# A decoder block on one core: up projection with both halves of the activations in one matmul, convolution over three blocks at a time, merge projections with tokens on the partition

## The chip, the core and the metric

The kernel runs on one core of a Trainium2 chip. The core has a matrix engine (PE, with its weight loads shown apart as PEld), a vector engine (DVE), a scalar engine (ACT), GpSimd (POOL) and a queue engine (SP) that issues most transfers. Matmul results go to PSUM; everything else lies in SBUF with 128 partitions. The metric is the device time of one execution in microseconds (us), and lower is better. [...]

## What is computed

One decoder layer for 256 tokens of 2048 channels, batch 1 (cut to what matters):

```python
h = rmsnorm(x, norm1_g) * (1 + sc1) + sh1            # sh1, sc1, g1, sh2, sc2, g2 = silu(c) @ w_ada + b_ada
proj = h @ w_in        # queries, keys, values, gates, GLU input (a, g), merge gates (ga, gb)
o_nsa = nsa_attention(q, kc, vc, ks, vs, kw, vw)     # 16 heads of 128, two key/value groups
y_a = o_nsa @ w_o_nsa
u = a * sigmoid(g)
u = causal_dwconv(u, conv_dw_w, width 31) + conv_dw_b
y_b = silu(layernorm(u)) @ conv_pw_w + conv_pw_b
merged = sigmoid(ga) * y_a + sigmoid(gb) * y_b
x = x + g1 * (merged @ w_out)
h = rmsnorm(x, norm2_g) * (1 + sc2) + sh2
u = causal_dwconv(h @ ffn_w_up, ffn_dw_w, width 3) + ffn_dw_b     # 2 * 5632 columns: a, g
x = x + g2 * ((silu(g) * a) @ ffn_w_down)
out = rmsnorm(x, final_g)
```

## The kernel before

The weights of the products, nearly 300 MB, are read once, in tiles of 128 partitions by up to 1024 columns (`wtile`, L202 to L215): SP issues the transfer of `raw`, ACT casts it to `hi` (L212), DVE subtracts to get `lo` (L213). `hi` and `lo` have three buffers each, so a cast waits until PE has finished with the tile three before it. (Up to the attention a fourth pair, from the pool `more`, takes every fourth tile.) Each product runs over the contraction in blocks of 128 (k) and holds its result in one of two PSUM accumulators.

There are two forms of product. `prod_x` puts tokens on the partition of the result: the activations are the loaded operand, the weights stream, up to 512 columns in one matmul, and each k takes 2 token blocks x 3 matmuls (L235 to L237). `prod_w` puts channels on the partition: 128 columns of weights are the loaded operand and the activations stream, 256 columns (the tokens), so that 512 columns of weights take 4 blocks x 3 matmuls for each k (L249, L251, L252). Activations are kept as two tiles, one of hi and one of lo.

The order of the work is that of the code, with three queues of background work (`heads_q`, `conv_q`, `ada_q`): after each weight tile `tick` takes items from them, as long as the costs written beside an item (ns of DVE, ACT, transfer) stay under what PE has been given. The instructions are then put in order at build time, for each engine apart, by a scheduler; weight casts have priority. On the chip each engine follows its own list in order.

The stages, with the time at which the first matmul of each starts: the shift and scale and the first GLU blocks (0 to 180 us), the rest of the GLU, keys, values and the first queries (to 416 us), the attention of 16 heads among the products of `q_chunk(2)`, `q_chunk(3)` and `gate_a` (to about 626 us), w_o_nsa, the gates gb and conv_pw_w (to 908 us), w_out (to 1013 us), and the feed-forward part in three pieces of up and down projection (to the end).

The depthwise convolution of 31 taps is background work from 182 us to 691 us: for each pair of channel blocks ACT makes the first term and DVE adds 30 taps to each block by one multiply-add over 256 tokens each (L446). The layer norm over channels follows, then its result is split into `uT` for conv_pw_w. In the attention, `scores(h)` makes the exponentials of head h and `values(h)` multiplies them with the values; `heads` puts the scores AHEAD = 2 heads before the values. Three of the four gates `gate_a` are made during the attention. The merge adds the two branches, channels on the partition, and splits the sum into `mT`, the loaded operand of w_out. The steps of `ada_steps` (L263 to L269) stream w_ada through DVE for the later shifts, scales and gates.

## Time and profile before

| | |
|---|---|
| three runs | 1781.09, 1782.22, 1783.61 us, median 1782.22 us |
| profiled execution, span from first to last instruction | 1779.5 us (its own time with what lies around the span is not listed) |
| PE busy | 97% of the span, 13252 matmuls |
| DVE busy | 71% |
| ACT busy | 48% |
| read from HBM | 402.80 MB, 228 GB/s over the span |
| granted TensorE clock, mean | 0.986 of full |

A busy time counts every moment in which an instruction of the engine was under way. Matmuls overlap, so the pace of PE is read from the starts of neighbouring matmuls and not from their durations. Idle time of an engine is put down to what ended it.

### The profile page before, as it was taken

The numbers are of one execution on the slowest core, as the hardware profiler recorded it, in microseconds if no ns is written. First come the engines' busy times: TensorE is split into PE (matmuls) and PEld (weight loads), VectorE is DVE, ScalarE is ACT, GpSimd is POOL, SyncE is SP. The second block draws the span as 40 slices with busy tenths as digits, with TensorE's granted clock in tenths as the row PEclk, the third lists the DMA queues.
The fourth block names the chain that finished last, engine by engine and source line by source line (L and its number), as shares of the span: only waits on it lengthen the run. The fifth ranks groups of instructions, "written<-read, shape, count | busy, mean of one in ns | idle before, by whom it ended". The sixth has DMA issues, their size and how long they took to land.

```text
span 1779.5 us, 32395 instructions
## 1 busy us (share of the span) xinstructions
PE 1726.8 (97%) x13252; PEld 1628.7 (92%) x13252; DVE 1268.8 (71%) x1808; ACT 845.5 (48%) x1168; POOL 5.5 (0%) x22
## 2 busy tenths in 40 slices
PE   5999999999999999999999899999999999999997
PEld 3777999899999999999988899998999998999986
DVE  2223999998999898877885666666556766576665
ACT  4333444344768644653344644444344454344453
POOL 0000000000000000000000000000000000000000
PEclk9989999999999999999999999999999999999998
DMA  9996777884764676799997576766676767666663
GB/s 307 358 334 221 225 226 230 272 283 135 240 195 130 210 240 202 243 325 308 308 312 234 177 234 205 219 207 227 207 219 207 220 205 223 206 176 186 181 190 127
DMA packets 225152, 407.01 MB, mean 229 GB/s; under 512 B 12876, under 2 KB 91500, under 8 KB 224364
## 3 DMA queue, kind: packets, MB, share of 16 engines
q1 hardware_dynamic: 223596, 400.49, 71.4%
q10 hardware_dynamic: 1408, 4.46, 0.7%
q8 instruction: 103, 1.69, 0.4%
q14 instruction: 45, 0.37, 0.1%
HBM read 402.80 MB, written 2.10 MB: 228 GB/s over the span
## 4 chain that ended last, share of the span: by engine, by line
PE 91%; DMA 3%; DVE 3%; ACT 1%; issue 1%; SPq 0%; DVEq 0%; ACTq 0%
PE accw L252 20%; PE accw L249 20%; PE accw L251 20%; PE accx L236 6%; PE accx L237 6%; PE accx L235 6%; DMA araw<-in_w_ada_dram 2%; PE pt L664 1%; PE pt L368 1%; DVE lo L213 1%; PE pt L703 1%; PE pt L398 1%; PE pt L399 1%; PE pt L400 1%; PE acc_g L398 1%
## 5 line engine op out<-in xcount | busy, mean ns | idle before, releaser
L212 ACT CAST hi<-raw 128x1024 fp32r<-128x1024 f32 (+2 forms) x562 | 574.5, 1023 | 816.1 <-PE accw L251 474.6
L213 DVE TENSOR_TENSOR lo<-raw,hi 128x1024 fp32r<-128x1024 f32 (+2 forms) x562 | 668.4, 1190 | 408.0 <-ACT hi L212 398.8
L252 PE MATMUL accw<-act,lo 128*128 128x256 f32 x3104 | 883.0, 285 | 1.3 <-DVE lo L213 1.3
L249 PE MATMUL accw<-act,hi 128*128 128x256 f32 x3104 | 882.7, 284 | 0.0
L251 PE MATMUL accw<-act,hi 128*128 128x256 f32 x3104 | 882.5, 284 | 0.0
L252 PEld LDWEIGHTS accw<-act,lo 128*128 128x128 f32 x3104 | 596.1, 192 | 4.1 <-issue 1.8
L249 PEld LDWEIGHTS accw<-act,hi 128*128 128x128 f32 x3104 | 596.4, 192 | 3.4 <-issue 2.6
L251 PEld LDWEIGHTS accw<-act,hi 128*128 128x128 f32 x3104 | 596.3, 192 | 2.4 <-issue 2.2
L236 PE MATMUL accx<-lo,act 128*128 128x512 f32 (+2 forms) x664 | 227.6, 343 | 1.0 <-DVE lo L213 1.0
L235 PE MATMUL accx<-hi,act 128*128 128x512 f32 (+2 forms) x664 | 227.0, 342 | 0.0
L237 PE MATMUL accx<-hi,act 128*128 128x512 f32 (+2 forms) x664 | 226.7, 342 | 0.0
L446 DVE SCALAR_TENSOR_TENSOR cacc<-big,cw,cacc 128x255 f32<-128x255 f32 (+24 forms) x480 | 201.2, 464 | 0.3
L269 DVE SCALAR_TENSOR_TENSOR t<-araw,cs,t 128x1024 f32<-128x1024 f32 x120 | 153.6, 1280 | 23.5 <-DMA araw<-in_w_ada_dram 23.5
L236 PEld LDWEIGHTS accx<-lo,act 128*128 128x128 f32 x664 | 125.8, 189 | 18.4 <-DVE lo L213 2.6
L235 PEld LDWEIGHTS accx<-hi,act 128*128 128x128 f32 x664 | 125.8, 189 | 14.5 <-ACT hi L212 0.2
L237 PEld LDWEIGHTS accx<-hi,act 128*128 128x128 f32 x664 | 125.8, 189 | 14.3 <-issue 0.4
L904 DVE SCALAR_TENSOR_TENSOR t<-accw,fw,t 128x255 f32<-128x255 f32 (+1 forms) x176 | 84.2, 479 | 2.5
L902 ACT ACTIVATE t<-accw,fw 128x256 f32<-128x256 f32 x88 | 49.3, 560 | 0.0
L368 PE MATMUL pt<-araw,cz 128*32 128x256 f32 x512 | 37.4, 404 | 9.7 <-DMA araw<-in_w_ada_dram 7.5
L318 DVE TENSOR_TENSOR act<-t,act 128x512 fp32r<-128x512 f32 x38 | 26.0, 686 | 18.3 <-ACT act L317 18.3
L368 PEld LDWEIGHTS pt<-araw,cz 128*32 128x32 f32 x512 | 12.9, 111 | 20.5 <-DMA araw<-in_w_ada_dram 5.8
L677 ACT ACTIVATE s<-s,st 128x128 f32<-128x128 f32 (+1 forms) x64 | 28.5, 447 | 1.4 <-DVE st L675 1.1
(208 smaller groups left out, 1035.6 us busy)
## 6 DMA issues: line engine op xcount, KB each, us to landing
araw<-in_w_ada_dram SPq DMA_DIRECT2D x192, 512.0 KB, 5.4
raw<-in_ffn_w_up_dram SPq DMA_DIRECT2D x176, 512.0 KB, 3.7
raw<-in_w_in_dram SPq DMA_DIRECT2D x116, 512.0 KB, 4.5
raw<-in_ffn_w_down_dram SPq DMA_DIRECT2D x88, 512.0 KB, 4.6
raw<-in_w_in_dram SPq DMA_DIRECT2D x48, 384.0 KB, 3.8
raw<-in_w_o_nsa_dram SPq DMA_DIRECT2D x32, 512.0 KB, 4.8
raw<-in_conv_pw_w_dram SPq DMA_DIRECT2D x32, 512.0 KB, 6.2
raw<-in_w_out_dram SPq DMA_DIRECT2D x32, 512.0 KB, 5.2
```

The costliest lines, as they stand in the source:

```text
L212: nc.scalar.copy(hi[:, :n], raw[:, :n])
L213: los.append(nc.vector.tensor_tensor(lo[:, :n], raw[:, :n], hi[:, :n], op=ALU.subtract).ins)
L235: nc.tensor.matmul(o, ah[:, k, s], hi, start=k == 0, stop=False)
L236: nc.tensor.matmul(o, ah[:, k, s], lo, start=False, stop=False)
L237: nc.tensor.matmul(o, al[:, k, s], hi, start=False, stop=k == nk - 1)
L249: nc.tensor.matmul(acc[:, b, :], hi[:, s], ah[:, k, :], start=k == 0 and b % 2 == 0, stop=False, skip_group_check=True)
L251: nc.tensor.matmul(acc[:, b, :], hi[:, s], al[:, k, :], start=False, stop=False, skip_group_check=True)
L252: nc.tensor.matmul(acc[:, b, :], lo[:, s], ah[:, k, :], start=False, stop=last, skip_group_check=True)
L269: nc.vector.scalar_tensor_tensor(acc, raw, cs[:, k:k + 1], acc, op0=ALU.mult, op1=ALU.add)
L368: nc.tensor.matmul(p_[32 * i:32 * i + 32, side, :], cz[:, k + i, :], raw[:, i, :], start=k == 0, stop=k == KB - 4, skip_group_check=True)
L446: nc.vector.scalar_tensor_tensor(acc[:, s:], u[:, b, :T - s], cw[:, CW - 1 - s, b:b + 1], acc[:, s:], op0=ALU.mult, op1=ALU.add)
L904: nc.vector.scalar_tensor_tensor(dst[:, j, s:], pp[:, j, :T - s], fw[:, 2 - s, b:b + 1], dst[:, j, s:], op0=ALU.mult, op1=ALU.add)
```

## The change

- `prod_p` is new and makes the up projection: hi and lo of the activations lie side by side in one tile `[P, KB, 2, T]`, so that one matmul of 512 columns takes weights hi x activations (hi | lo), and a second one of 256 columns adds weights lo x activations hi. It makes 256 columns of weights at a time (their transfers have rows of 1 KB instead of 2 KB); hi and lo sums meet in `ffn_conv`, by a copy on ACT and an addition on DVE.
- The four gates ga, w_o_nsa, the four gates gb and conv_pw_w become `prod_x`. The merge has tokens on the partition, takes the bias of conv_pw_w from a transfer that repeats it on all partitions, and is turned by 32 transposes (`turn_m`), three and four weight tiles after the end of each of the four merge products (`coming`).
- The convolution takes three blocks at a time (one group has one block). For 16 of 31 taps (`WIDE`) ACT makes the products of the blocks into one tile `cprod` with a single buffer, and DVE adds it to all three blocks at once; for 14 taps DVE does what it did.
- AHEAD becomes 1. The fourth pair of `hi` and `lo` before the attention is gone. The gate `g1b` gets its place when the convolution is done, and its 32 ada steps enter the queue there at a transfer cost of 1500.

```diff
-AHEAD = 2
+AHEAD = 1
...
-    acts = ctx.enter_context(tc.tile_pool(name="acts", bufs=4))
+    acts = ctx.enter_context(tc.tile_pool(name="acts", bufs=2))
...
-        return acts.tile([P, KB, T], F32R, tag="act", name=nm("act"))
+        return acts.tile([P, KB, 2, T], F32R, tag="act", name=nm("act"))
...
     def tick():
+        for c in coming:
+            c[0] -= 1
+        while coming and coming[0][0] <= 0:
+            coming.popleft()[1]()
...
-        turn[0] += 1
-        pool, bufs = (ext[0], 1) if ext[0] is not None and turn[0] % 4 == 0 else (wp, 3)
-        hi = pool.tile([P, WT], F32R, tag="hi", name=nm("hi"), bufs=bufs)
-        lo = pool.tile([P, WT], F32R, tag="lo", name=nm("lo"), bufs=bufs)
+        hi = wp.tile([P, WT], F32R, tag="hi", name=nm("hi"))
+        lo = wp.tile([P, WT], F32R, tag="lo", name=nm("lo"))
...
+    def prod_p(act, src, c0):
+        acc = ps_acc.tile([P, 2, 2, T], F32, tag="acc", name=nm("accp"))
+        for k, hi, lo in tiles(src, KB, c0, 2 * P):
+            for b in range(2):
+                s = slice(b * P, (b + 1) * P)
+                nc.tensor.matmul(acc[:, b], hi[:, s], act[:, k], start=k == 0, stop=False, skip_group_check=True)
+                nc.tensor.matmul(acc[:, b, 0, :], lo[:, s], act[:, k, 0, :], start=False, stop=k == KB - 1,
+                                 skip_group_check=True)
+        return acc
...
+    WIDE = (3, 5, 7, 9, 11, 13, 15, 17, 19, 21, 23, 25, 27, 29, 30, 1)
...
+        def product(b, s):
+            def f():
+                if b == b0:
+                    box["p"] = cvp.tile([P, n, T], F32, tag="cprod", name=nm("cprod"))
+                    if s == 1:
+                        nc.gpsimd.memset(box["p"][:, :, 0:1], 0.0)
+                nc.scalar.mul(box["p"][:, b - b0, s:], u[:, b, :T - s], cw[:, CW - 1 - s, b:b + 1])
+            return f
+        def wide(s):
+            def f():
+                acc, prod = box["a"], box["p"]
+                if s == 1:
+                    nc.vector.tensor_add(u[:, b0:b0 + n, :], acc, prod)
+                else:
+                    nc.vector.tensor_add(acc[:, :, s:], acc[:, :, s:], prod[:, :, s:])
+            return f
...
+        narrow = deque(({"dve": 470}, tap(b, s)) for s in range(2, CW) if s not in WIDE for b in blk)
+        each = -(-len(narrow) // len(WIDE))
+        for s in WIDE:
+            conv_q.extend(({"act": 500}, product(b, s)) for b in blk)
+            conv_q.extend(narrow.popleft() for _ in range(min(each, len(narrow))))
+            conv_q.append(({"dve": 170 + n * 265}, wide(s)))
...
-        gp = prod_w(h1, w_in, C_MA + n * 512, 512)
+        gp = prod_x(h1, w_in, C_MA + n * 512, 512)
...
-        yp = prod_w(oT, w_o_nsa, n * 512, 512)
-        nc.vector.tensor_mul(merged[:, 4 * n:4 * n + 4, :], yp, sg)
+        yp = prod_x(oT, w_o_nsa, n * 512, 512)
+        nc.vector.tensor_mul(merged[:, :, n * 512:(n + 1) * 512], yp, sg)
...
+    def turn_m(b):
+        def f():
+            p_ = pt([P, 2, T])
+            for j in range(2):
+                for t in range(NT):
+                    nc.tensor.transpose(p_[:, j, t * P:(t + 1) * P], merged[:, t, (b + j) * P:(b + j + 1) * P], ident)
+            split(mT[:, b:b + 2], p_)
...
-        yp = prod_w(uT, conv_pw_w, n * 512, 512)
...
+        yp = prod_x(uT, conv_pw_w, n * 512, 512)
+        y = t4([P, NT, 512])
+        for t in range(NT):
+            nc.vector.tensor_add(y[:, t, :], yp[:, t, :], bias)
+            nc.vector.tensor_mul(y[:, t, :], y[:, t, :], gbs[:, t, s])
+            nc.vector.tensor_add(merged[:, t, s], merged[:, t, s], y[:, t, :])
+        coming.extend([3 + i, turn_m(4 * n + 2 * i)] for i in range(2))
...
     def ffn_conv(pp, b0, dst):
-        for j in range(4):
+        v = t4([P, 2, T])
+        nc.scalar.copy(v, pp[:, :, 1, :])
+        nc.vector.tensor_add(v, v, pp[:, :, 0, :])
+        for j in range(2):
...
-            pg = prod_w(h2, ffn_w_up, FFN + (b0 + i) * P, 512)
+            pg = prod_p(h2, ffn_w_up, FFN + (b0 + i) * P)
```

Where the instructions stand: first PE in the second product of the up projection, before the change (accw is the accumulator, act the two activation tiles, hi and lo the weights).

```order
L249 MATMUL accw_11472<-act_11107,hi_11474 128x256
L251 MATMUL accw_11472<-act_11108,hi_11474 128x256
L252 MATMUL accw_11472<-act_11107,lo_11475 128x256
L249 MATMUL accw_11472<-act_11107,hi_11474 128x256
L251 MATMUL accw_11472<-act_11108,hi_11474 128x256
L252 MATMUL accw_11472<-act_11107,lo_11475 128x256
```

And the same two blocks after it:

```order
L263 MATMUL accp_9996<-act_9791,hi_9998 128x512
L264 MATMUL accp_9996<-act_9791,lo_9999 128x256
L263 MATMUL accp_9996<-act_9791,hi_9998 128x512
L264 MATMUL accp_9996<-act_9791,lo_9999 128x256
```

Two matmuls of 256 columns have become one of 512, and the third stays.

Second, DVE among the GLU products, where the convolution begins (cacc is its sum, cprod ACT's products, t a sum of ada steps), before:

```order
L213 TENSOR_TENSOR lo_1785<-raw_1783,hi_1784 128x768
L213 TENSOR_TENSOR lo_1813<-raw_1811,hi_1812 128x768
L446 SCALAR_TENSOR_TENSOR cacc_1668<-big_191,cw,cacc_1668 128x253
L446 SCALAR_TENSOR_TENSOR cacc_1674<-big_191,cw,cacc_1674 128x253
L213 TENSOR_TENSOR lo_1839<-raw_1837,hi_1838 128x768
L446 SCALAR_TENSOR_TENSOR cacc_1668<-big_191,cw,cacc_1668 128x252
L446 SCALAR_TENSOR_TENSOR cacc_1674<-big_191,cw,cacc_1674 128x252
L213 TENSOR_TENSOR lo_1869<-raw_1867,hi_1868 128x768
```

After:

```order
L467 SCALAR_TENSOR_TENSOR cacc_1667<-big_190,cw,cacc_1667 128x250 x3
L216 TENSOR_TENSOR lo_1846<-raw_1844,hi_1845 128x768
L486 TENSOR_TENSOR cacc_1667<-cacc_1667,cprod_1787 128x3x249
L216 TENSOR_TENSOR lo_1879<-raw_1877,hi_1878 128x768
L467 SCALAR_TENSOR_TENSOR cacc_1667<-big_190,cw,cacc_1667 128x248 x3
L216 TENSOR_TENSOR lo_1904<-raw_1902,hi_1903 128x768
L486 TENSOR_TENSOR cacc_1667<-cacc_1667,cprod_1870 128x3x247
L216 TENSOR_TENSOR lo_1935<-raw_1933,hi_1934 128x768
```

Every second tap of three blocks is now one addition (L486) that needs ACT's cprod, and it stands between the weight tiles.

Third, PE at the values of the last but two head. Before, it stands among the products of the third gate (L698 to L700 are transposes of the exponentials, L703 and L704 the values, L664 the scores, accw_6516 the gate):

```order
L252 MATMUL accw_6516<-act_189,lo_6755 128x256
L703 MATMUL pt_6057<-t_869_6063,big_3235 128x256
L704 MATMUL pt_6057<-t_869_6063,big_3235 128x128
L664 MATMUL pt_6091<-big_3235,big_3898 128x2x128
L664 MATMUL pt_6093<-big_3235,big_3898 128x512
L703 MATMUL pt_6057<-t_871_6071,big_3235 128x256
L704 MATMUL pt_6057<-t_871_6071,big_3235 128x128
L249 MATMUL accw_6516<-act_189,hi_6754 128x256
L251 MATMUL accw_6516<-act_190,hi_6754 128x256
L695 MATMUL pt_6146<-big_3235 128x256
```

After (L700 scores, L739 and L740 values, accx_6637 the first product with w_o_nsa, act_4631 the heads' results):

```order
L239 MATMUL accx_6637<-hi_6763,act_4631 128x512
L739 MATMUL pt_6073<-t_921_6079,big_3276 128x256
L740 MATMUL pt_6073<-t_921_6079,big_3276 128x128
L700 MATMUL pt_6107<-big_3276,big_3960 128x2x128
L700 MATMUL pt_6109<-big_3276,big_3960 128x512
L739 MATMUL pt_6073<-t_923_6087,big_3276 128x256
L740 MATMUL pt_6073<-t_923_6087,big_3276 128x128
L731 MATMUL pt_6149<-big_3276 128x256
L237 MATMUL accx_6829<-hi_6831,act_4631 128x512
L734 MATMUL pt_6151<-ident,s_6054 128x128
```

Among the values of head 12 stood the scores of head 15, and now stand those of head 14. The third gate has ended by then: the values of all of the last eight heads stand behind it, among the first two products with w_o_nsa, whose k-th block needs the result of head k.

## Rows read from the trace of the kernel before

**Rows 1.** The page: busy time by engine, and TensorE's granted clock in 40 slices.

```profile
PE 1726.8 (97%) x13252; PEld 1628.7 (92%) x13252; DVE 1268.8 (71%) x1808; ACT 845.5 (48%) x1168; POOL 5.5 (0%) x22
...
PEclk9989999999999999999999999999999999999998
```

**Rows 2.** The chain that ended last, shares of the span by engine.

```profile
PE 91%; DMA 3%; DVE 3%; ACT 1%; issue 1%; SPq 0%; DVEq 0%; ACTq 0%
```

**Rows 3.** Timeline of PE in the up projection: start us, duration us, instruction.

```profile
1099.73 0.28 PE L249 MATMUL accw<-act,hi 128*128 128x256 f32 x1
...
1100.69 0.28 PE L252 MATMUL accw<-act,lo 128*128 128x256 f32 x1
```

**Rows 4.** Timeline of PE in the down projection, columns as before.

```profile
1224.78 0.39 PE L236 MATMUL accx<-lo,act 128*128 128x512 f32 x1
...
1226.60 0.39 PE L235 MATMUL accx<-hi,act 128*128 128x512 f32 x1
```

**Rows 5.** Busy time by stage: window, length, engines (instructions), PE clock, DMA share, GB/s.

```profile
165.00:415.00 250.00, 248.00 (x2059) 239.27 (x2060) 222.07 (x389) 109.00 (x135) 1.29 (x4) 0.99 0.78 238
415.83:649.52 233.69, 233.69 (x1762) 222.40 (x1761) 212.27 (x432) 150.04 (x327) 0.53 (x1) 0.99 0.60 187
...
814.55:908.35 93.80, 93.45 (x769) 92.15 (x767) 78.16 (x82) 36.75 (x39) 0.00 (x0) 1.00 0.90 307
...
1012.76:1779.50 766.74, 754.32 (x5563) 721.27 (x5561) 497.58 (x574) 359.73 (x430) 0.00 (x0) 0.99 0.65 200
```

**Rows 6.** The chain in order of time, attention: start us, us, what.

```profile
431.10 0.44 PE pt L645 x4
431.54 1.72 PE pt L664 x6
...
452.68 0.43 PE pt L703 x2
```

**Rows 7.** Groups by line and shape, 415 to 650 us, ACT's work for the heads.

```profile
L677 ACT ACTIVATE s<-s,st 128x256 f32<-128x256 f32 x32 | 15.9, 500 | 0.1
L702 ACT COPY t<-pt 128x384 f32<-128x384 f32 x32 | 14.5, 472 | 9.1 <-PE pt L700 8.9
L693 ACT ACTIVATE s<-s,st 128x256 f32<-128x256 f32 x32 | 14.4, 497 | 0.0
L677 ACT ACTIVATE s<-s,st 128x128 f32<-128x128 f32 x32 | 12.6, 394 | 1.2 <-DVE st L675 1.1
...
L677 ACT ACTIVATION_READ_ACCUMULATOR s<-s,st 128x1 f32 x64 | 12.1, 188 | 0.0
L693 ACT ACTIVATE s<-s,st 128x128 f32<-128x128 f32 x32 | 11.1, 395 | 1.2 <-DVE st L683 1.1
...
L317 ACT CAST act<-pt 128x256 fp32r<-128x256 f32 x16 | 5.9, 369 | 12.5 <-PE pt L704 12.4
```

**Rows 8.** Who waited for whom, 415 to 650 us: total, times, longest.

```profile
ACT hi L212 <- PE accw L251: 44.4, 28, 4.0
```

**Rows 9.** Groups of the whole span, DVE and ACT: busy us, mean ns.

```profile
L212 ACT CAST hi<-raw 128x1024 fp32r<-128x1024 f32 x476 | 499.3, 1050 | 685.5 <-PE accw L251 428.0 <-PE accx L237 165.7 <-issue 72.1
...
L213 DVE TENSOR_TENSOR lo<-raw,hi 128x768 fp32r<-128x768 f32 x48 | 45.6, 954 | 10.0 <-ACT hi L212 6.4 <-PE pt L400 3.3
...
L864 DVE TENSOR_TENSOR big<-big,t 128x512 f32<-128x512 f32 x12 | 8.1, 683 | 0.0
```

**Rows 10.** The page's groups: the taps of the convolution before.

```profile
L446 DVE SCALAR_TENSOR_TENSOR cacc<-big,cw,cacc 128x255 f32<-128x255 f32 (+24 forms) x480 | 201.2, 464 | 0.3
```

**Rows 11.** Transfers from 1200 to 1250 us, rows of 2 KB and more.

```profile
DMA packets 5434, 11.25 MB, mean 225 GB/s; under 512 B 345, under 2 KB 345, under 8 KB 5430
...
q1 hardware_dynamic: 5430, 11.20, 68.6%
```

**Rows 12.** Transfers from 1250 to 1268 us, nearly all rows of 1 KB.

```profile
DMA packets 3605, 4.01 MB, mean 223 GB/s; under 512 B 119, under 2 KB 3454, under 8 KB 3603
...
q1 hardware_dynamic: 3603, 3.98, 70.9%
```

More of the change, by code (lines that the diff above doesn't have):

```diff
@@ L315, in split @@
     def split(dst, src):
-        hi, lo = dst
+        hi, lo = (dst[:, :, 0, :], dst[:, :, 1, :]) if len(dst.shape) == 4 else (dst[:, 0, :], dst[:, 1, :])
         nc.scalar.copy(hi, src)
@@ L397, in glu_first @@
             s = slice(b * P, (b + 1) * P)
-            nc.tensor.matmul(o, hi[:, 0, s], h1[0][:, k, :], start=k == 0 and not second, stop=False, skip_group_check=True)
-            nc.tensor.matmul(o, hi[:, 0, s], h1[1][:, k, :], start=False, stop=False, skip_group_check=True)
-            nc.tensor.matmul(o, lo[:, 0, s], h1[0][:, k, :], start=False, stop=k == KB - 1, skip_group_check=True)
+            nc.tensor.matmul(o, hi[:, 0, s], h1[:, k, 0, :], start=k == 0 and not second, stop=False, skip_group_check=True)
+            nc.tensor.matmul(o, hi[:, 0, s], h1[:, k, 1, :], start=False, stop=False, skip_group_check=True)
+            nc.tensor.matmul(o, lo[:, 0, s], h1[:, k, 0, :], start=False, stop=k == KB - 1, skip_group_check=True)
     with tc.tile_pool(name="first", bufs=4) as first:
@@ L731, in block_kernel, with conv_done @@
         drain(heads_q)
-    late = ctx.enter_context(tc.tile_pool(name="late", bufs=1))
-    g1b = late.tile([P, D], F32, name="gb", tag="gb")
-    for i in range(2):
-        ada_q.extendleft(reversed(ada_steps(2 * D + i * WT, to_bcast(g1b, 2 * D, i), PACE)))
+    gate1 = {}
+    def conv_done():
+        cv.__exit__(None, None, None)
+        late = ctx.enter_context(tc.tile_pool(name="late", bufs=1))
+        gate1["b"] = late.tile([P, D], F32, name="gb", tag="gb")
+        for i in range(2):
+            ada_q.extendleft(reversed(ada_steps(2 * D + i * WT, to_bcast(gate1["b"], 2 * D, i), 1500)))
+    conv_q.append(({}, conv_done))
     lb = {}
```

118 lines of the change are left out of this document (52 added, 66 removed).

## The prediction

> **What bounds the kernel now.** I read the busy times first: PE 97% of the span, DVE 71%, ACT 48%, the clock full in nearly every slice [rows 1]. A busy PE alone proves little, because matmuls overlap; but the chain that ended last runs on PE for 91% of the span [rows 2]. So I looked at PE's pace. In the up projection nine neighbouring matmuls of 256 columns start within 0.96 us, 120 ns apart [rows 3]; in the down projection nine of 512 columns start within 1.82 us, 227 ns apart [rows 4]. So two matmuls of 256 columns cost 240 ns and one of 512 costs 227. A line through both pairs gives 107 ns for 256 columns and 13 ns for each matmul, whatever its length. The stages show no other bound for long: in the last 767 us PE is busy for 754, DVE for 498 and ACT for 360 [rows 5]. Two places are tight besides: the attention (416 to 650 us), where DVE is busy for 212 of 234 us, and 815 to 908 us, where the transfers' share is 0.90 [rows 5].
>
> **The up projection.** 88 blocks of 128 columns times 16 blocks of k are 1408 triples of matmuls. A triple took 3 x 120 = 360 ns; one of 512 columns and one of 256 take 227 + 120 = 347. 13 ns x 1408 = **-18.3 us**. What comes on top lies beside PE: 44 products each get a copy on ACT and an addition of 512 elements on DVE, 0.68 us [rows 9], 30 us in all. DVE then has 498 + 30 of some 748 us, ACT about 360 + 30: cover enough; without it each addition would cost its 0.68 us. The weights now come in rows of 1 KB. The stretch of the down projection that already reads such rows moves 223 GB/s at a share of 70.9% [rows 12], the stretch before it 225 GB/s at 68.6% with longer rows [rows 11]: 4% more engine time for each byte. With the faster PE the last stage's 0.65 [rows 5] becomes 0.65 x 360/347 x 1.04 = 0.70. I cost it at nothing; if it were no longer hidden, PE would wait on transfers at most as now at a share of 0.90.
>
> **Sixteen products with tokens on the partition.** For 512 columns and one k, 12 matmuls of 256 columns (1440 ns) become 6 of 512 (1362 ns): 78 ns, times 16 k, times 16 products: **-20.0 us** (a product falls from 23.0 to 21.8 us). The loaded operand and the streamed one trade places, which rows 3 and 4 show in both forms at these paces.
>
> The trace can be set against a rule here. By the Trainium skill, "TensorE: Matmul & The Clock Gate", section "Back-to-back issue gap", a matmul of N columns at the full clock follows the last after N / 2.4 + 2.5 ns. That would make a matmul less worth 2.5 ns, and the 1408 + 1536 that go worth 7.4 us instead of the 38.3 us above; the sum below would end at 1784 us. The trace does not agree: 120 ns stand where the rule gives 109 [rows 3]. I go by the rows.
>
> **The merge.** 32 transposes come onto PE. Four of 128 columns take 0.44 us [rows 6]: 32 x 0.11 = **+3.5 us** (7 if they fall into a stretch at half clock). They stand three and four weight tiles into the next product, so that PE should not wait for the sum. DVE gets six operations of 512 elements for each merge product, 6 x 0.68 = 4.1 us [rows 9], beside a product of 21.8 us, about what it did before. The transfers there go from 0.90 to 0.90 x 23.0/21.8 = 0.95. Close, but not over; if they bind, the 5 us that the four merge products gain are lost.
>
> **The convolution.** DVE loses 16 of 30 taps of 16 blocks: 480 operations in 201 us become 224, at 0.42 us 94 us [rows 10]. It gains 80 additions over three blocks, 0.95 us each as the subtraction of 768 elements [rows 9], and 16 over one, in all about 82 us. So DVE has some 25 us less. ACT gets 256 products of about 0.5 us, the price of its scaling of 256 elements [rows 7]: 127 us, in a stretch (165 to 650 us) where it has 109 + 150 of 484 us [rows 5]. PE was the bound there already, so I count no gain for DVE's 25 us. The new wait is this: cprod has one buffer, so ACT's next product waits for DVE's addition, and the weight casts stand behind it on ACT. Cover: a cast itself waits for PE to free a buffer (44 us in the attention stretch alone [rows 8]), and two finished tiles lie ahead, over 5 us at 23 us for eight tiles. Cost 0 is my value; the upper bound is a rival below.
>
> **The attention.** Ahead of a head's transposes now stands one head's work less. By the order, the values of all of the last eight heads come after the third gate. From the values of head 8 to those of head 15, PE has 130 matmuls of w_o_nsa products (29.5 us at 227 ns) and some 26 us of the heads themselves (scores of a head 1.29 us, from six for 1.72; values about 2.4 us [rows 6]): 55.5 us. ACT has in the same stretch 12 weight casts at 1.05 us [rows 9], 24 exponentials, 24 reads of their sums, 24 scalings, 16 copies and 8 casts of results at 0.50 and 0.39, 0.19, 0.50 and 0.40, 0.47 and 0.37 us [rows 7], and 18 products of the convolution at up to 0.50: 12.6 + 10.7 + 4.5 + 10.7 + 7.6 + 3.0 + 8.9 = 58 us. So ACT is the longer by 2.5 us, with no waits counted, where before PE was busy throughout [rows 5]. Each head also needs a way round: scores, exponentials on ACT, scalings on ACT, transposes, copies, values. I take **+6 us**; lower bound 0, upper bound 2 us for each of the eight heads, 16 us.
>
> **Sum.** 1779.5 (span) - 18.3 - 20.0 + 3.5 + 6 = 1750.7 us. The span of the profiled execution is 2.7 us under the median of the runs, 1782.2, and I add this as what lies around it: **1753 us**.
>
> **Rivals.**
> - *The forecast*, with the attention at 0 to 14 us and the merge's transfers at 0 to 5: 1747 to 1764. Chance 0.62.
> - *ACT becomes the bound from 165 to 690 us.* For: 127 us more on an engine that follows its list in order, and AHEAD = 1. Against: half of its time was free there, and most of its waiting was for PE. If the attention loses its 16 us and the exchange of products in the convolution another 5 to 10 us, the time is near 1770 (1764 to 1778). Chance 0.17.
> - *Slower: the single cprod buffer.* Each of 96 additions on DVE waits for the last of ACT's products, which waits for the addition before. If 0.5 us of this (one product [rows 7]) shows on PE each time, it is 48 us: 1753 + 48 = 1801. It decides from 29 / 96 = 0.3 us on. For: DVE is busy for 222 of the 250 us from 165 us on, and can make up little. Against: in the order one to two weight tiles (2.2 to 2.9 us of PE) stand between two additions. Chance 0.09.
> - *The fixed cost is not of each matmul.* If the 512-column matmul, between matmuls of 256, starts the next one 240 ns later and not 227, the up projection gains nothing: 1771. Against it stand the starts between neighbours of 512 columns [rows 4]; no row is for it. Chance 0.03.
> - *Better*: no wait at all in the attention, and DVE's 25 us end some of the old ones: under 1747, near 1742. PE has only 2 us idle of 250 ahead of the attention [rows 5], so there is little to end. Chance 0.09.
>
> **How the numbers follow.** About 0.2%, 3.6 us, is what a measurement of this kernel can tell from no change. Faster is the forecast, the better case, the fixed-cost case and nearly all of the second: 0.62 + 0.09 + 0.03 + 0.14 = 0.88. Same, 1778.6 to 1785.8, takes the end of the second: 0.03. Slower: 0.09. The predicted time is that of the likeliest case. The range leaves out the slower case, the end of the second and half of the better one: 1742 to 1775, with some 0.83 inside.
>
> **What would show it.** Right: in the up projection starts 227 and 120 ns apart in turn, and a last stage (from the first up matmul to the end) about 18 us shorter; four gates, w_o_nsa and merge products of 21.8 us where PE does nothing else; DVE under 90% from 165 to 416 us. Wrong: casts on ACT that wait for DVE's additions or for the convolution's products, with PE waiting for lo or hi behind them; PE idle between the heads by more than 2 us each; transposes of the merge at twice their time; weights of the up projection landing late.

## The result and the profile after

The changed kernel takes 1769.8 us in the median of four runs (1767.07 to 1772.41), the kernel before 1781.65 us. The ratio is 0.993, with a 95% interval of 0.9914 to 0.9946; in a second comparison it was 0.9932 (0.9917 to 0.9946). So it is faster, by some 12 us, where the forecast was 29: the time lies inside the range, but at less than half of the gain.

The page of the changed kernel, busy times and the chain that ended last by engine, which answer to [rows 1, 2]:

```profile
PE 1705.5 (96%) x10340; PEld 1476.0 (83%) x10340; DVE 1268.9 (72%) x1692; ACT 968.3 (55%) x1465; POOL 6.1 (0%) x28
...
PE 83%; DVE 6%; DMA 5%; ACT 3%; issue 2%; SPq 0%; DVEq 0%; ACTq 0%
```

PE has some 2900 matmuls less but is busy for only 21 us less, and the chain now leaves PE for 17% of the span instead of 9%. The windows by stage, columns as in [rows 5], cut at the first matmul of the same products; first the rows of the kernel before that [rows 5] leaves out:

```profile
649.52:742.51 92.99, 92.99 (x775) 92.88 (x773) 82.74 (x107) 41.84 (x42) 0.00 (x0) 1.00 0.72 221
742.51:814.55 72.04, 71.13 (x583) 69.97 (x581) 55.71 (x50) 43.05 (x50) 0.00 (x0) 1.00 0.87 305
...
908.35:1012.76 104.41, 98.83 (x545) 85.75 (x543) 71.78 (x98) 47.63 (x67) 0.00 (x0) 0.97 0.77 250
```

And after the change:

```profile
165.00:417.33 252.33, 248.88 (x2065) 239.99 (x2066) 211.54 (x312) 159.03 (x260) 2.25 (x7) 0.99 0.78 235
417.33:656.63 239.30, 233.54 (x1283) 197.92 (x1281) 203.53 (x363) 186.52 (x422) 0.73 (x3) 0.97 0.57 179
656.63:744.69 88.06, 88.06 (x388) 72.97 (x389) 77.87 (x92) 51.38 (x65) 0.10 (x1) 1.00 0.74 231
744.69:820.70 76.01, 69.52 (x293) 55.80 (x292) 61.04 (x55) 43.32 (x50) 0.00 (x0) 0.98 0.90 316
820.70:916.00 95.30, 94.39 (x429) 76.70 (x428) 83.42 (x86) 37.63 (x39) 0.00 (x0) 1.00 0.93 324
916.00:1017.87 101.87, 96.06 (x529) 83.52 (x527) 69.03 (x94) 46.48 (x66) 0.00 (x0) 0.98 0.71 235
1017.87:1770.40 752.53, 739.70 (x4152) 643.95 (x4152) 514.90 (x618) 386.95 (x486) 0.00 (x0) 0.99 0.65 204
```

Set against the same stages of the two profiled executions (1779.5 and 1770.4 us); the last column is a second profiled execution of the changed kernel (`after_again`, 1770.0 us):

| stage | before, us | after, us | difference | by the forecast's terms | after, once more |
|---|---|---|---|---|---|
| to the attention | 415.8 | 417.3 | +1.5 | 0 | 414.7 |
| attention: 5 of the 16 products | 233.7 | 239.3 | +5.6 | -6.2 + 6 | 238.2 |
| the next 4 products | 93.0 | 88.1 | -4.9 | -5.0 | 88.1 |
| merge: 7 products and w_out | 270.3 | 273.2 | +2.9 | -8.8 + 3.5 | 273.3 |
| feed-forward part | 766.7 | 752.5 | -14.2 | -18.3 | 755.7 |

Only the third row came out as forecast, and it is the one stage after the change in which PE is never idle (88.06 of 88.06 us). The misses are 8.2 us in the merge, 5.8 in the attention, 4.1 in the feed-forward part and 1.5 ahead of the attention, where the second execution has none. PE's idle time, the length of a stage less its busy time, grew from nothing to 5.8 us in the attention and from 6.8 to 13.2 us in the merge.

**The up projection.** A product of two float32 operands is summed from hi x hi, hi x lo and lo x hi of their two parts; L263, the matmul of 512 columns of each pair, makes the first two, and L264 the third. A timeline of PE, L263 alone, first in the first piece, then in the second; the outer rows of each are 20 pairs apart:

```profile
1099.92 0.40 PE L263 MATMUL accp<-act,hi 128*128 128x512 f32 x1
...
1106.85 0.40 PE L263 MATMUL accp<-act,hi 128*128 128x512 f32 x1
```

```profile
1399.74 0.40 PE L263 MATMUL accp<-act,hi 128*128 128x512 f32 x1
...
1406.81 0.40 PE L263 MATMUL accp<-act,hi 128*128 128x512 f32 x1
```

6.93 us for 20 pairs is 346.5 ns, as forecast. 7.07 us is 353.5 ns, and it stays so through all 512 pairs of the second piece, with nothing waiting and the clock full. Over the trace, the starts in the first piece follow one another in a cycle of two pairs (231 + 112, 233 + 117 ns), in the third piece of one (230 + 117) and in the second of three (241 + 120, 235 + 114, 232 + 118). The second piece is the one that PE enters straight from the down projection, with nothing between.

**The attention.** PE and ACT in their timelines, from the moment in which PE has nothing more to do (L713 exponentials of the next head, L215 weight casts, L477 products of the convolution, L331 the cast of a finished head's result, L237 the product with w_o_nsa that needs it):

```profile
588.90 0.27 PE L736 MATMUL pt<-ident,s 128*128 128x128 f32 x1
593.78 0.79 PE L237 MATMUL accx<-hi,act 128*128 128x512 f32 x1 [4.60 <-ACT act L331]
```

```profile
587.24 1.28 ACT L713 ACT_TABLE_LOAD   x1
588.53 0.40 ACT L713 ACTIVATE s<-s,st 128x128 f32<-128x128 f32 x1
...
589.32 1.98 ACT L215 CAST hi<-raw 128x1024 fp32r<-128x1024 f32 x2
591.20 0.51 ACT L713 ACTIVATE s<-s,st 128x256 f32<-128x256 f32 x1
...
591.71 0.49 ACT L713 ACTIVATE s<-s,st 128x256 f32<-128x256 f32 x1
...
592.20 1.27 ACT L477 ACTIVATE cprod<-big,cw 128x249 f32<-128x249 f32 x3
593.38 0.35 ACT L331 CAST act<-pt 128x256 fp32r<-128x256 f32 x1
```

ACT does not pause. The 0.35 us cast for which PE waits stands behind a table load, the exponentials of the next head, two weight casts and three products of the convolution. Behind this wait the granted clock was at half, the level of 1.2 GHz, until 600.0 us:

```profile
593.10:600.00 6.90, 6.22 (x15) 4.46 (x16) 3.84 (x11) 4.81 (x15) 0.00 (x0) 0.51 0.41 146
```

In all 13.7 us of this stage ran at that level (from 425.9, 548.8 and 593.1 us on), against 6.8 us before the change (from 421.8 us on). An estimate from these rows: 239.3 us less 5.8 us of idle time and half of 13.7 us is 226.7 us, where the kernel before has 233.7 less half of 6.8, 230.3 us. So by this estimate PE's own pace gained 3.6 of the 6.2 us; waits and the lower clock took 9.2 us.

**The merge.** The waits of PE from gate gb 1 to the end of conv_pw_w (total, times, longest), before and after:

```profile
PE accw L252 <- DVE lo L213: 1.3, 2, 0.9
```

```profile
PE accx L238 <- DVE lo L216: 5.2, 5, 2.2
PE accx L237 <- ACT hi L215: 2.2, 1, 2.2
```

DVE at the first of them (L216 makes lo, L282 is an ada step, L831 the four scalings of the layer norm):

```profile
752.70 1.22 DVE L216 TENSOR_TENSOR lo<-raw,hi 128x1024 fp32r<-128x1024 f32 x1
753.84 1.28 DVE L282 SCALAR_TENSOR_TENSOR t<-araw,cs,t 128x1024 f32<-128x1024 f32 x1
755.03 4.63 DVE L831 TENSOR_TENSOR big<-big,t 128x1024 f32<-128x1024 f32 x4
759.57 1.22 DVE L216 TENSOR_TENSOR lo<-raw,hi 128x1024 fp32r<-128x1024 f32 x1
```

From 753.84 to 759.57 us DVE does other work than lo, and PE waits 2.2 us, until 760.85 us. The second wait of 2.2 us is for a weight cast that stands on ACT behind four swishes of the norm (L837) and two casts of its result (L331). The third, again 2.2 us, is for a lo that stands on DVE behind an ada step, which itself waited 2.60 us for its transfer:

```profile
766.27 2.08 ACT L837 ACTIVATE big<-big,par 128x256 f32<-128x256 f32 x4
...
768.25 1.98 ACT L331 CAST act<-big 128x1024 fp32r<-128x1024 f32 x2
...
770.13 1.05 ACT L215 CAST hi<-raw 128x1024 fp32r<-128x1024 f32 x1
...
771.23 0.50 PE L237 MATMUL accx<-hi,act 128*128 128x512 f32 x1 [2.16 <-ACT hi L215]
771.43 1.29 DVE L282 SCALAR_TENSOR_TENSOR t<-araw,cs,t 128x1024 f32<-128x1024 f32 x1 [2.60 <-DMA araw<-in_w_ada_dram]
...
773.90 0.69 PE L238 MATMUL accx<-lo,act 128*128 128x512 f32 x1 [2.17 <-DVE lo L216]
```

Before the change DVE's run without lo was as long (5.7 us, from 748.32 to 754.06 us: the same four scalings and an ada step), and PE's longest wait for lo was 0.9 us. What is new is not the run but that the faster PE gets to its end sooner:

```profile
748.32 4.63 DVE L790 TENSOR_TENSOR big<-big,t 128x1024 f32<-128x1024 f32 x4
```

### The profile page after: what moved, and what is told of

Read it like the earlier page. It is cut to its first block, busy times and chain, and to the rows that moved or that the text cites. A ratio compares the mean times of both kernels' runs of the same rounds, so it can differ in the third digit from the quotient of the medians.

```text
span 1770.4 us, 26852 instructions
## 1 busy us (share of the span) xinstructions
PE 1705.5 (96%) x10340; PEld 1476.0 (83%) x10340; DVE 1268.9 (72%) x1692; ACT 968.3 (55%) x1465; POOL 6.1 (0%) x28
## 3 DMA queue, kind: packets, MB, share of 16 engines
q1 hardware_dynamic: 268652, 400.49, 70.6%
## 4 chain that ended last, share of the span: by engine, by line
PE 83%; DVE 6%; DMA 5%; ACT 3%; issue 2%; SPq 0%; DVEq 0%; ACTq 0%
PE accp L263 18%; PE accx L238 11%; PE accx L239 11%; PE accx L237 11%; PE accp L264 9%; PE accw L253 4%; PE accw L252 4%; PE accw L250 4%; DMA araw<-in_w_ada_dram 3%; DVE lo L216 2%; DVE t L282 1%; PE pt L381 1%; PE pt L700 1%; DMA raw<-in_w_in_dram 1%; ACT hi L215 1%
## 5 line engine op out<-in xcount | busy, mean ns | idle before, releaser
L215 ACT CAST hi<-raw 128x1024 fp32r<-128x1024 f32 (+2 forms) x562 | 575.1, 1024 | 675.6 <-PE accx L239 287.0
L216 DVE TENSOR_TENSOR lo<-raw,hi 128x1024 fp32r<-128x1024 f32 (+2 forms) x562 | 668.7, 1191 | 379.1 <-ACT hi L215 365.7
L263 PE MATMUL accp<-act,hi 128*128 128x512 f32 x1408 | 492.2, 395 | 0.2 <-DVE act L332 0.2
L238 PE MATMUL accx<-lo,act 128*128 128x512 f32 (+2 forms) x1176 | 431.7, 367 | 7.0 <-DVE lo L216 6.9
L237 PE MATMUL accx<-hi,act 128*128 128x512 f32 (+2 forms) x1176 | 430.9, 367 | 7.2 <-ACT act L331 4.6
L239 PE MATMUL accx<-hi,act 128*128 128x512 f32 (+2 forms) x1176 | 429.3, 365 | 0.0
L264 PE MATMUL accp<-act,lo 128*128 128x256 f32 x1408 | 393.7, 280 | 0.3 <-DVE lo L216 0.3
L263 PEld LDWEIGHTS accp<-act,hi 128*128 128x128 f32 x1408 | 264.0, 188 | 62.7 <-DVE act L332 0.8
L264 PEld LDWEIGHTS accp<-act,lo 128*128 128x128 f32 x1408 | 265.5, 189 | 0.9 <-DVE lo L216 0.6
L237 PEld LDWEIGHTS accx<-hi,act 128*128 128x128 f32 x1176 | 222.8, 189 | 43.6 <-ACT act L331 4.8
L253 PE MATMUL accw<-act,lo 128*128 128x256 f32 x672 | 191.5, 286 | 0.7 <-DVE lo L216 0.7
L252 PE MATMUL accw<-act,hi 128*128 128x256 f32 x672 | 192.1, 286 | 0.0
L250 PE MATMUL accw<-act,hi 128*128 128x256 f32 x672 | 192.0, 286 | 0.0
L282 DVE SCALAR_TENSOR_TENSOR t<-araw,cs,t 128x1024 f32<-128x1024 f32 x120 | 153.6, 1280 | 24.0 <-DMA araw<-in_w_ada_dram 23.9
L253 PEld LDWEIGHTS accw<-act,lo 128*128 128x128 f32 x672 | 129.3, 193 | 3.1 <-issue 1.9
L252 PEld LDWEIGHTS accw<-act,hi 128*128 128x128 f32 x672 | 129.5, 193 | 1.8 <-issue 1.7
L250 PEld LDWEIGHTS accw<-act,hi 128*128 128x128 f32 x672 | 129.5, 193 | 0.9 <-issue 0.9
L477 ACT ACTIVATE cprod<-big,cw 128x253 f32<-128x253 f32 (+15 forms) x256 | 109.7, 487 | 20.2 <-DVE cacc L486 20.0
L486 DVE TENSOR_TENSOR cacc<-cacc,cprod 128x753 f32<-128x753 f32 (+22 forms) x90 | 73.7, 819 | 3.5 <-ACT cprod L477 2.2
```

Source lines behind the costliest of these rows:

```text
L215: nc.scalar.copy(hi[:, :n], raw[:, :n])
L216: los.append(nc.vector.tensor_tensor(lo[:, :n], raw[:, :n], hi[:, :n], op=ALU.subtract).ins)
L237: nc.tensor.matmul(o, act[:, k, 0, s], hi, start=k == 0, stop=False)
L238: nc.tensor.matmul(o, act[:, k, 0, s], lo, start=False, stop=False)
L239: nc.tensor.matmul(o, act[:, k, 1, s], hi, start=False, stop=k == nk - 1)
L250: nc.tensor.matmul(acc[:, b, :], hi[:, s], act[:, k, 0, :], start=k == 0 and b % 2 == 0, stop=False, skip_group_check=True)
```

## The experiments

All ratios are to the kernel before on the same chip, with 95% intervals; "stage" is the length in the profiled execution.

**The up projection alone** (`up_only`): the kernel before with

```diff
-            pg = prod_w(h2, ffn_w_up, FFN + (b0 + i) * P, 512)
+            pg = prod_p(h2, ffn_w_up, FFN + (b0 + i) * P)
```

and what goes with it (hi and lo in one tile, the sum in `ffn_conv`).

> The kernel before with the up projection of the change alone (hi and lo side by side, prod_p, the sum in ffn_conv); all else as before. The forecast's price (347 ns for a pair of matmuls instead of 360 ns for a triple) gives 18.3 us less: 1763 to 1764. The theory from the changed kernel's trace, that a row of alternating matmuls of 512 and 256 columns can settle into more than one rhythm (346.6 ns a pair in the first and third piece there, 353.3 ns in the second), gives 14 to 18 us less, 1764 to 1768, with a rhythm that may be another in another piece or execution. Rival: the second piece is slow for a reason of its own (its transfers, its place in memory), then it is 353.3 ns in the second piece here too and 346.6 in the others.

Ratio 0.9906 (0.9891 to 0.9921), 1766.5 against 1784.1 us: -17.6 us. The pairs took 346.7, 353.3 and 346.7 ns in the three pieces, which makes 15.3 us; in the profile the feed-forward part fell from 766.7 to 751.9 us, by 14.8. The interval of the whole, 14.1 to 19.4 us, holds both. By the medians more than the whole gain of the change lies here. The three paces are also what the rival foretold, a second piece that is slow for a reason of its own; the order inside the pair, below, speaks against it. By the formula of the Trainium skill that the prediction set aside ("TensorE: Matmul & The Clock Gate", section "Back-to-back issue gap"), an estimate of 1408 x 2.5 ns = 3.5 us was to be had. The section itself keeps the formula for a single matmul and says that in a stream of weight loads and matmuls both set the spacing, so that it counts too little at few columns, as the trace shows at 256 (120 ns, not 109), and too much at 512, where the trace does not agree (227 ns, not 216).

**All but the up projection** (`no_up`): the changed kernel with the up projection of before.

```diff
-            pg = prod_p(h2, ffn_w_up, FFN + (b0 + i) * P)
+            pg = prod_w(h2, ffn_w_up, FFN + (b0 + i) * P, 512)
```

> The changed kernel with the up projection of before (prod_w over 512 columns, three matmuls of 256 columns); all else as changed. If the up projection's gain is its own and does not depend on the rest: 14 to 18 us above the changed kernel, 1784 to 1788, so the rest of the change together loses 2 to 6 us against the kernel before. Rival: the rest is neutral and the up projection brought all of the 12 us: 1782.

1.0016 (1.0001 to 1.0031): the rest of the change, whose terms sum to -10.5 us in the forecast, costs some 3 us. Its attention, the same instructions as in the changed kernel, took 234.9 us and not 239.3, with 5.6 us of idle time but only 6.8 us at half clock:

```profile
417.30:652.20 234.90, 229.26 (x1282) 194.78 (x1280) 202.92 (x363) 186.53 (x422) 0.73 (x3) 0.99 0.58 182
```

So some 3 of the 4.4 us between the two are, by an estimate from these rows (half of the 6.9 us that run at half clock only in the changed kernel's trace), the clock's alone, and attention stages of single executions are told apart only beyond that.

**The order inside the pair** (`up_2_and_2`, the changed kernel; `up_22`, the kernel before with the up projection alone):

```diff
-                nc.tensor.matmul(acc[:, b], hi[:, s], act[:, k], ...)
-                nc.tensor.matmul(acc[:, b, 0, :], lo[:, s], act[:, k, 0, :], ...)
+                nc.tensor.matmul(acc[:, b], hi[:, s], act[:, k], ...)
+            for b in range(2):
+                s = slice(b * P, (b + 1) * P)
+                nc.tensor.matmul(acc[:, b, 0, :], lo[:, s], act[:, k, 0, :], ...)
```

> The changed kernel with the order inside prod_p changed: for each k two matmuls of 512 columns (one for each block), then two of 256; same matmuls, same operands. If the slow rhythm belongs to the strict alternation of 512 and 256: a pair takes 346.6 to 347 ns in all three pieces, the second piece's up projection takes 177.6 us instead of 180.9, total 1766 to 1768. Rival, the slow rhythm comes with any mix of lengths: a piece at 353 ns a pair remains, total within 2 us of the changed kernel. If other neighbours have a price of their own, more than 353 ns: slower.

> The kernel before with the up projection alone, in the order two of 512, two of 256 columns for each k. If this order avoids the slow rhythm wherever it stands: 348.3 ns a pair in all three pieces, 16.5 us less than before, 1763 to 1766, with less spread between executions than the kernel with strict alternation. Rival, no difference from the alternating order: 0.990 to 0.992 of before.

0.9928 (0.9909 to 0.9948) and 0.9903 (0.9884 to 0.9921). The second piece of `up_22`, in a timeline of L265 (two matmuls of 512 columns in each row, the outer rows 20 pairs apart):

```profile
1400.06 0.63 PE L265 MATMUL accp<-act,hi 128*128 128x512 f32 x2
...
1407.02 0.63 PE L265 MATMUL accp<-act,hi 128*128 128x512 f32 x2
```

6.96 us, 348 ns a pair, and the same in all pieces of both kernels, the second too, where 346.6 to 347 ns were expected of `up_2_and_2`: the slow cycle belongs to the strict alternation and not to the second piece. The piece falls from 180.9 to 178.3 us; the two others grow by up to 0.7, so that nothing that can be measured is won over the alternation.

**The merge projections undone** (`old_merge`): the changed kernel with gates, w_o_nsa and conv_pw_w as `prod_w`, no transposes.

```diff
-        yp = prod_x(oT, w_o_nsa, n * 512, 512)
+        yp = prod_w(oT, w_o_nsa, n * 512, 512)
```

> The changed kernel with gates, w_o_nsa and conv_pw_w in the form of before (prod_w, channels on the partition, no transposes, no repeated bias); the rest as changed. If transfers set the pace of the merge (742 to 1013 us), the products there do not become longer in time: the eight products ahead of it cost 8 x 1.25 = 10 us, the merge gives back 0 to 6 us (no transposes, no bias transfer): 1774 to 1780. Rival, the merge's time is lost in the transposes and in DVE's order: the same stage is at most that of before, 270 us, and it shows no DVE waiting for transfers. If the merge form did bring the 16.5 us forecast: 1786.

0.9962 (0.9948 to 0.9976). Against 0.993 with them, the sixteen products brought some 6 us, transposes included, not 16.5. The stage of the merge is 275.3 us with the old products and 273.2 with the new: PE waited 6.0 us for lo there too.

**The convolution undone** (`old_conv`), **AHEAD alone** (`ahead1`, the kernel before) and both undone (`old_conv_ahead2`):

```diff
-        for s in WIDE:
-            conv_q.extend(({"act": 500}, product(b, s)) for b in blk)
+        conv_q.extend(({"dve": 390}, tap(b, s)) for s in range(1, CW) for b in bs)
```

```diff
-AHEAD = 2
+AHEAD = 1
```

> The changed kernel with the convolution of before (pairs of blocks, all taps on DVE, no products on ACT); AHEAD stays 1. If ACT's products of the convolution are what makes ACT late in the attention (PE waited 4.8 us there for a cast of a head's result), the attention falls from 239 us to 228 to 234: total 1759 to 1766. Rival, AHEAD = 1 alone makes the heads late: the attention stays at 237 to 241 us and the total at 1768 to 1772. If DVE becomes the bound again in its place (25 us more of taps): slower, 1772 to 1780.

> The kernel before with AHEAD = 1 and nothing else. The theory now held: the attention's loss comes from AHEAD = 1, not from the convolution's products on ACT, for with the old convolution the changed kernel's attention was as long (240.4 us against 239.3). Then the attention here is 238 to 243 us instead of 233.7, and the total is 4 to 9 us above the kernel before. Rival, it is the exchange of the activations' form or the order after the third gate that delays w_o_nsa's first products: the attention stays at 233 to 235 us and the total within 2 us of before.

> The changed kernel with the convolution of before and AHEAD = 2. If AHEAD = 1 is what costs the attention its time: the attention falls from 240 us to 226 to 232 and the total to 1758 to 1763. If not, the total stays at 1768 to 1772 as with the old convolution alone.

`old_conv` 0.9924 (0.9909 to 0.9939), attention 240.4 us; `ahead1` 1.0019 (1.0009 to 1.003), attention 240.2 us instead of 233.7, with 4.0 us of idle time where there was none (row below); `old_conv_ahead2` 0.9917 (0.9901 to 0.9933), attention 237.3 us. So my first theory, that ACT's products make the heads late, fell: without them the attention is no shorter. AHEAD = 1 costs 6.5 us beside the old products, but putting AHEAD back gives only 3 us beside the new ones, less than `no_up` differs from the changed kernel with the same attention.

```profile
415.20:655.40 240.20, 236.15 (x1762) 224.14 (x1761) 211.94 (x429) 151.39 (x328) 0.53 (x1) 0.98 0.58 181
```

The single cprod buffer shows on ACT, in the page's group of its products (idle time before them, and what ended it):

```profile
L477 ACT ACTIVATE cprod<-big,cw 128x253 f32<-128x253 f32 (+15 forms) x256 | 109.7, 487 | 20.2 <-DVE cacc L486 20.0
```

20 us of waits on ACT are not 20 us on PE: with the old convolution the total is only 1 us lower. Not run: AHEAD = 2 beside the changed convolution, a second cprod buffer, and the fourth pair of hi and lo or the old place of g1b by themselves in the changed kernel.

**No convolution at all** (`no_conv`): taps, products and additions left out.

> The changed kernel without the taps of the convolution (first terms, products, additions left out; the norm works on the unconvolved values). If the attention is long because DVE and ACT have the convolution's work beside the heads: the stage from 417 to 657 us falls from 239 us to 225 to 229 (PE's own pace there is 224.6 us). Rival, the way round of a head with AHEAD = 1 and the order behind the third gate set it, whatever else runs: it stays at 234 us or more. The total: 1745 to 1758 by the first, 1762 to 1768 by the second.

0.9911 (0.9896 to 0.9926). Its attention in the windows:

```profile
413.70:644.20 230.50, 229.32 (x1283) 196.56 (x1282) 148.99 (x246) 145.45 (x316) 0.53 (x1) 0.99 0.58 184
```

With 55 us less on DVE and 41 less on ACT the same matmuls take 230.5 us, still with AHEAD = 1. So the convolution's work beside the heads, which `old_conv` only moved from ACT to DVE, is what keeps the faster products from showing, but not all of it: 227.5 us were forecast without waits. Nor does the whole kernel gain as much. The norm and the ada steps of g1b, which follow the convolution, move forward, and the next four products take 102.9 us instead of 88.1, with 8.8 us of waits for lo:

```profile
644.20:747.10 102.90, 94.09 (x394) 73.98 (x393) 95.48 (x94) 54.98 (x62) 0.00 (x0) 0.98 0.88 299
```

**Transfers in the merge** (`pace_3500`: more of w_ada before the merge; `ada_half`: 16 of 32 transfers for g1b left out, all operations kept):

```diff
-PACE = 5000
+PACE = 3500
```

```diff
-                raw = wp.tile([P, WT], F32, tag="araw", ...)
-                nc.sync.dma_start(raw, w_ada[k * P:(k + 1) * P, c0:c0 + WT])
+                if k % every == 0:
+                    raw = box["raw"] = wp.tile([P, WT], F32, tag="araw", ...)
+                    nc.sync.dma_start(raw, w_ada[k * P:(k + 1) * P, c0:c0 + WT])
+                raw = box["raw"]
```

> The changed kernel with PACE 3500 instead of 5000, so that more of the background transfers of w_ada (0.5 MB each) go ahead of 650 us and fewer fall into the merge. If transfers set the merge's pace: 10 to 17 fewer transfers of w_ada between 742 and 916 us, 5 to 9 MB of 54.9, and that stretch falls from 171 us to 160 to 165, the total to 1760 to 1765 unless the attention loses. Rival, DVE's order or the transposes set the pace: the stretch stays at 168 to 172 us though it moves fewer bytes. If the transfers come in the way earlier: the attention grows by 3 us or more and the total stays.

> The changed kernel with every second transfer of w_ada for the gate g1b left out (16 of 32; its row block is used twice, so that part of the computation is changed); every operation on DVE, ACT and PE stays. These 8.4 MB fall mostly between 742 and 916 us. If transfers set the pace of the merge: that stretch falls from 171 us to 158 to 163 (some 46 to 49 MB), near the 152.5 us of its seven products, and the total by 8 to 12 us, to 1758 to 1762. Rival, the order of DVE's work or the transposes set it: DVE has the same work, the stretch stays at 168 us or more and the total within 3 us of the changed kernel.

`pace_3500` 1.0 (0.999 to 1.001): the merge falls from 273.2 to 266.6 us, but the attention grows from 239.3 to 254.1, with two waits of 7.6 us each behind the heads' DVE and ACT work. `ada_half` 0.9941 (0.9925 to 0.9956). Its stretch from gate gb 1 to the end of conv_pw_w in the windows, and PE's waits there:

```profile
742.50:910.90 168.40, 162.14 (x722) 131.52 (x722) 147.06 (x143) 80.91 (x89) 0.00 (x0) 1.00 0.85 290
```

```profile
PE accx L238 <- DVE lo L216: 4.8, 4, 2.5
PE accx L237 <- ACT hi L215: 1.5, 1, 1.5
```

The transfers' share fell from 0.92 to 0.85 and the stretch only from 171.3 to 168.4 us; 6.3 of 7.4 us of waits stayed. The theory that transfers set the pace of the merge fell. They have a part in it: the third of the waits shown above, behind the ada step, was 0.8 us here instead of 2.2.

**The norm's end at higher stated costs** (`ln_spread`, the changed kernel; a higher stated cost is meant to deal the operations out more widely), and **the changed kernel once more** (`after_again`):

```diff
-LN_SILU = 1500
-LN_SPLIT = 2500
+LN_SILU = 3000
+LN_SPLIT = 4000
...
-    [(1130, 0, ln_scale(j + 1))] * (j < 3)
+    [(3000, 0, ln_scale(j + 1))] * (j < 3)
```

> The changed kernel with dearer stated costs for the end of the layer norm (LN_SILU 3000 instead of 1500, scaling 3000 instead of 1130, LN_SPLIT 4000 instead of 2500), so that these operations are dealt out over more weight tiles; same operations. With half of the transfers for g1b left out, the stretch from gate gb 1 to the end of conv_pw_w still took 168.4 us of which PE waited 8, so transfers alone are out; the theory now is that PE waits in the merge behind the norm's bursts on DVE (four scalings in a row, 4.6 us) and ACT (eight swishes in a row, 4.0 us). Then the waits of 745 to 916 us fall from 11.0 us to 3 to 6 and the total to 1762 to 1766. Rival, the waits belong to transfers and bursts together or move with the bursts: 8 us or more of waits stay, total within 2 us of the changed kernel.

> The changed kernel once more, on the same chip as the other three, for a comparison without the spread between chips. 0.992 to 0.995 of before; waits of PE as in the first profile (attention 12 to 15 us over its own pace, merge 9 to 12 us) if they come from the order of the work, other places if they are chance.

0.991 (0.989 to 0.993) and 0.9932 (0.9917 to 0.9946). PE's waits in the same stretch of `ln_spread`:

```profile
PE accx L237 <- ACT hi L215: 1.8, 1, 1.8
PE accx L238 <- DVE lo L216: 1.5, 4, 0.8
```

3.3 us are left of 7.4, and the first part of the merge takes 70.6 us instead of 76.0, with the transfers' share still at 0.90. The median fell by 3.7 us, but the intervals overlap. The scalings themselves were not dealt out; all four still stand in a row on DVE:

```profile
752.04 1.22 DVE L216 TENSOR_TENSOR lo<-raw,hi 128x1024 fp32r<-128x1024 f32 x1
753.18 4.63 DVE L831 TENSOR_TENSOR big<-big,t 128x1024 f32<-128x1024 f32 x4
757.72 1.22 DVE L216 TENSOR_TENSOR lo<-raw,hi 128x1024 fp32r<-128x1024 f32 x1
```

What the edit changed is the order around them. No ada step joins the run any more, so that DVE goes without a lo for 4.5 us and not 5.7 (753.84 to 759.57 us in the changed kernel). On ACT casts of the norm's result alternate with weight casts, and the longest stretch without a weight cast fell from 6.8 to 5.3 us. PE's wait at the scalings fell from 2.2 to 0.2 us. In `after_again` the waits stand at the same places (5.3 us for a head's cast, until 590 us; 2.6, 1.4 and 2.5 us between 755 and 770 us): they come from the order of the work. What does change is the first piece of the up projection, 182.7 us there, with 353.4 ns a pair.

**A better version** (`up_merge`, `up_merge_ln`): the kernel before with the up projection (two and two) and the merge projections, but its own convolution, AHEAD = 2 and place of g1b; then the same with the stated costs of `ln_spread`.

> The kernel before with the up projection (in the order two of 512, two of 256) and the merge projections of the change, but its own convolution, AHEAD = 2, fourth pair of hi and lo and place of g1b. By the stages measured so far: up projection -16.5 us, the four products from 650 to 742 us -5 us, the attention between 0 and -4 us, the merge (742 to 1013 us) between +2 and -4 us. Total 1754 to 1762, under both the changed kernel and the kernel with the up projection alone. Rival, the merge's form gains nothing beside heads and transfers: 1763 to 1767, as the up projection alone.

> The kernel before with the up projection and the merge projections of the change, as run already, and the norm's end dealt out over more weight tiles. If bursts are what costs the merge: 3 to 5 us under the same kernel without it (0.9936 of before), 0.990 to 0.992. Compared with the up projection alone on the same chip: if the merge projections bring anything, this one is faster; rival, beside heads, norm and transfers they bring nothing and the two are equal within 2 us.

0.9936 (0.9923 to 0.9949) (1754 to 1762 us were expected, 1768.6 measured) and **0.9872 (0.9852 to 0.9892), 1761.6 us, 22 us less than before**: the fastest kernel of all. The two were measured on different chips, but their intervals lie apart, so the raised costs are a gain here; the four scalings stand in a row on DVE in both. The two profiled executions show only 3.0 us of it, in the merge (272.5 and 269.5 us). Its waits of PE in the merge, where the old products had 1.3 us:

```profile
PE accx L246 <- DVE lo L223: 1.9, 3, 0.8
```

On the same chip the up projection alone stood at 0.9903, 1764.8 us: by the medians the sixteen products and the norm's costs are together worth 3 us beside it, though the intervals overlap a little; without those costs the products lost (0.9936). Those costs beside the old products were not run. In the attention they bring nothing even now (236.8 and 239.9 us against 233.7).

## Why the prediction was right or wrong

The steps in their order:

- **The up projection, -18.3 us.** Right in its mechanism: the fixed cost is of each matmul. The term was mis-sized: the feed-forward part fell by 14.8 us in `up_only` (-17.6 us over the whole kernel, 14.1 to 19.4), by 14.2 in the changed kernel and by 11.0 in `after_again`, where the first piece had the slow pace too. The 227 and 120 ns were read from rows of one length each [rows 3, 4]; in alternation a pair settles into 346.7 or 353.3 ns. 512 pairs at 6.6 ns are the 3.4 us that the second piece lost. Cover on DVE and ACT and the 1 KB rows were right: a share of 0.65, below the forecast 0.70, and 0.5 us of waits of PE in this part.
- **Sixteen products, -20.0 us.** This is the step that failed. 78 ns for each k is true, but it is the price of PE's time, and I took it off the end everywhere. It counted in full in four products, where PE is busy without a gap. In the five of the attention and the seven of the merge most of it turned into waits for lo, hi and the heads' results and, in the attention, into half clock: by the estimate above 9.2 of the 11.8 us lost against the sum without waits in the attention, and 6.4 of 8.2 in the merge, as idle time of PE. The rest, 2.6 and 1.8 us, stays open. Undone, the sixteen cost 6 us and not 16.5.
- **The merge.** The transposes cost what was said. The price of 0 to 5 us for transfers was bounded by their share, 0.90 [rows 5], and that was the wrong thing to look at: 6.4 of the 8.2 us lost are idle time of PE, two of the three largest waits stand behind the norm's operations on DVE and ACT, and another order of these gave back 3.6 us of the stage in `ln_spread` (269.6 us). DVE's average there, 144 of 171 us, hides 5.7 us in a row without a lo. How much of the rest belongs to transfers is open: one wait stood behind an ada step that was itself waiting for its transfer, and `ada_half` and `pace_3500` moved fewer bytes and gained 3.8 and 6.6 us over the whole merge, and the second changed the order of DVE's work as well.
- **The attention, +6 us.** ACT was indeed late behind the third gate, with the wait where the text put it. The price was 11.8 us over the sum without waits, inside the bound of 16; the text counted ACT's work and the way round, but not the 6.8 us at half clock that followed the wait. AHEAD = 1 alone explains 6.5 in the kernel before; beside the new products the stage takes 235 to 241 us whichever AHEAD and convolution it has (254 in `pace_3500`, with more of w_ada in it), and 230.5 only without the convolution.
- **The convolution, 0.** Nearly right: the GLU products ahead of the keys take 104.9 us instead of 103.9, and undoing it changes the total by 1 us, inside the intervals. DVE fell to 84% of the stretch from 165 us on. Of ACT's 20.0 us of waits for cprod no more than that 1 us is to be seen: the slower rival did not come.

The likeliest case was wrong; the second one, with ACT late in the attention, named the time (1764 to 1778) but only a part of the cause.

## What to carry to other kernels

In this kernel fewer matmul instructions were a gain in full only where PE has no gap. Elsewhere PE's faster pace takes away the cover of the engines that feed it, and most of what was saved came back as waits; so the gain is to be summed stage by stage, and for each stage the longest run of background operations on DVE and ACT between two weight tiles is to be set against the tiles that lie ahead, not the average load. Beside the up projection alone (0.9903), the stated costs of the norm, and with them the order of that work, decided whether the new products gained or lost: 0.9872 with the raised costs, 0.9936 without.

## What was not expected of the hardware

A row of alternating matmuls of 512 and 256 columns has more than one steady rhythm, 346.7 and 353.3 ns a pair, each kept for hundreds of pairs with the same instructions. In every trace of this order the second piece, which PE enters straight from the down projection, had the slow one; the third, whose first product is broken after one matmul by four others (L307), had the fast one; the first had either (346.7 ns in the first trace of the changed kernel, 353.4 in `after_again`). What decides it is not settled. Two and two in turn had one rhythm, 348.3 ns.

The granted clock fell without any wait of PE: in the changed kernel, after 28 matmuls of 15 columns in a row (L645, from 545.6 to 548.7 us), it was 0.52 of full from 548.6 to 551.9 us, the level of 1.2 GHz, while matmuls of 512 columns started 0.43 us apart. The kernel before had the same at 421.8 us, behind matmuls of 1 and 15 columns. The row after the change:

```profile
548.60:551.90 3.30, 3.30 (x10) 2.62 (x11) 2.85 (x13) 2.35 (x6) 0.00 (x0) 0.52 0.32 122
```
